# Sharing ten late rows between VectorE and GpSimd in a row-maximum kernel

## The chip, the cores and the metric

One core of a Trainium2 chip runs the kernel alone. The metric is the device time of one execution in microseconds (us). A few tenths of a microsecond lie between executions of one kernel, so a median is quoted with its range, and kernels are compared through a ratio with a 95% interval. The profile belongs to one execution and covers a slightly shorter stretch than the device time (162.6 us for 164.43 us before the change). All times inside a trace are counted from the start of that stretch.

## The reference

```
x: (32, 512, 1024) float32          # 16384 rows of 1024 numbers
out = max(x, axis=-1)               # (32, 512) float32
```

64 MiB (67.11 MB) come in, 64 KiB go out. Each of the 128 partitions owns 128 rows. In this document "a row" means one row on each partition: 128 x 1024 numbers, 512 KB.

## The kernel before

The rows come in as loads of decreasing size into a ring buffer of 46 rows. A load lands when its last byte is there. VectorE reduces each load. Near the end five full rows are spared it: TensorE turns such a row in eight 128 x 128 blocks into PSUM, ScalarE copies it back to SBUF, GpSimd takes the maximum over the partitions (an all-reduce), and TensorE turns one row of that result back into a PSUM column, from which VectorE takes a small reduction, called the merge below. The last row comes in two halves, the maximum of the first standing as one more number in front of the second.

```
BLOCKS = [[15, 15, 15, 13, 13, 11, 9, 9, 6, 6],      # rows per load
          [3, 3, 2, 1, 1, 1, 1, 1, 1, 1]]            # and one row in halves
BY_GPSIMD = {8: 1, 9: 3, 12: 1}                      # load: full rows for GpSimd
MERGE = {9: 8, 15: 9, 18: 12}                        # after load: merge of load
...
def turn(j, k):
    for c in range(C):                               # C = 8
        transpose(out=ps[:, c*P:(c+1)*P], in_=rows[:, k, c*P:(c+1)*P])   # TensorE
    nc.scalar.copy(out=sb, in_=ps)
    nc.gpsimd.partition_all_reduce(top, sb, P, max)
def back(j, k):
    for c in range(C):
        transpose(out=backs[j][:, k, c:c+1], in_=top[0:1, c*P:(c+1)*P])  # TensorE
...
for n in loads:
    nc.sync.dma_start(out=xc, in_=xb[:, b:b+n, :])
    ...
    nc.vector.reduce_max(out=cols[:, :n-m], in_=xc[:, :n-m, :])
    if j in MERGE:
        nc.vector.reduce_max(out=tiles[i][1], in_=backs[i])
...
nc.sync.dma_start(out=half, in_=xb[:, b, :H])
nc.sync.dma_start(out=tail[:, PAD:], in_=xb[:, b, H:])
nc.vector.reduce_max(out=tail[:, PAD-1:PAD], in_=half)
nc.vector.reduce_max(out=res[:, I-1:], in_=tail[:, PAD-1:])
```

## Time and profile before

| | |
|---|---|
| time, first 3 runs | 164.29 us (164.24 to 164.38) |
| loads, landings | 22; first at 21.44 us, last at 159.10 us |
| VectorE | ends at 160.36 us, 1.26 us after the last landing |
| end of the profile | 162.6 us, after the store |

### The profile page before, as it was taken

Reading aid. Unit: us, or ns where it says so; the run is one execution under the profiler, and the core shown is the slowest. Engines: PE = TensorE matmul, PEld = TensorE weight load, DVE = VectorE, ACT = ScalarE, POOL = GpSimd, SP = SyncE. Lnnn points to the kernel's source line nnn. Section 1 sums busy time; section 2 is a strip of 40 time slices with the busy share of each in tenths; the row PEclk is TensorE's granted clock in tenths of the full one; section 3 lists DMA queues with packets and bytes.
Section 4 is the critical chain, followed back from the end, with each engine's and each line's share of the span. In section 5 each row is a group of like instructions: output and inputs, shape, how many; then the busy total and the mean of one; then the engine's idle time right before and its main releaser. Section 6 shows DMA issues by size and latency. Waiting matters only on the chain.

```text
span 162.6 us, 293 instructions
## 1 busy us (share of the span) xinstructions
PE 13.0 (8%) x80; PEld 11.7 (7%) x80; DVE 135.0 (83%) x33; ACT 6.3 (4%) x6; POOL 16.3 (10%) x9
## 2 busy tenths in 40 slices
PE   0000000000000000000000000000000040943520
PEld 0000000000000000000000000000000030933420
DVE  3000079995999779999996999999999999999994
ACT  3000000000000000000000000000000011240200
POOL 0000000000000000000000000000000007099910
PEclk9999999999999999999999999999999999985555
DMA  7999699988999799999998989999999999999990
GB/s 242 484 484 438 287 484 484 484 378 348 484 484 484 333 498 432 445 419 419 419 419 387 499 388 427 417 426 408 417 435 435 471 399 426 423 418 409 406 368 16
DMA packets 3456, 67.18 MB, mean 413 GB/s; under 512 B 640, under 2 KB 640, under 8 KB 1792
## 3 DMA queue, kind: packets, MB, share of 16 engines
q1 hardware_dynamic: 3168, 67.11, 96.6%
q10 hardware_dynamic: 288, 0.07, 0.2%
HBM read 67.11 MB, written 0.07 MB: 413 GB/s over the span
## 4 chain that ended last, share of the span: by engine, by line
DVE 54%; DMA 44%; SPq 0%; issue 0%
DVE res L139 53%; DMA ring<-in_x_dram 44%; DVE res L156 0%; DVE tail L155 0%; SPq L133 0%; DVE res L143 0%
## 5 line engine op out<-in xcount | busy, mean ns | idle before, releaser
L139 DVE TENSOR_REDUCE res<-ring 128x1 f32<-128x1024 f32 (+6 forms) x20 | 132.1, 6653 | 24.3 <-DMA ring<-in_x_dram 24.3
L106 POOL PARTITION_ALL_REDUCE top<-sb x5 | 16.1, 3255 | 138.8 <-ACT sb L104 138.8
L98 PE MATMUL ps<-ident,ring 128*128 128x128 f32 x40 | 8.1, 382 | 134.2 <-DMA ring<-in_x_dram 131.8
L98 PEld LDWEIGHTS ps<-ident,ring 128*128 128x128 f32 x40 | 7.1, 204 | 134.3 <-issue 134.2
L104 ACT COPY sb<-ps 128x1024 f32<-128x1024 f32 x5 | 5.1, 1013 | 144.9 <-PE ps L98 143.0
L115 PE MATMUL fetched<-ident,top 1*128 1x1 f32 x40 | 5.0, 243 | 9.1 <-POOL top L106 9.1
L115 PEld LDWEIGHTS fetched<-ident,top 1*128 1x128 f32 x40 | 4.6, 214 | 10.3 <-POOL top L106 9.8
L104 ACT ACT_TABLE_LOAD x1 | 1.3, 1283 | 0.7 <-PEq L176 0.7
L76 DVE MEMSET ident<- 128x128 f32 x1 | 0.2, 165 | 0.8 <-PEq L176 0.8
L156 DVE TENSOR_REDUCE res<-tail 128x1 f32<-128x513 f32 x1 | 0.7, 686 | 0.0
L155 DVE TENSOR_REDUCE tail<-ring 128x1 f32<-128x512 f32 x1 | 0.7, 675 | 0.0
L83 DVE TENSOR_SCALAR rowno<-rowno 32x1 f32<-32x1 f32 x3 | 0.4, 147 | 0.1
L143 DVE TENSOR_REDUCE res<-fetched 128x1 f32<-128x8 f32 (+1 forms) x3 | 0.5, 161 | 0.0
L78 DVE TENSOR_TENSOR_SCAN colno<-ident 128x128 f32<-128x128 f32 x1 | 0.4, 425 | 0.0
L85 DVE TENSOR_SCALAR ident<-colno,rowno 128x128 f32<-128x128 f32 x1 | 0.3, 287 | 0.0
L80 DVE STREAM_TRANSPOSE rowno<-colno 128x32 f32<-128x32 f32 x1 | 0.2, 211 | 0.0
L176 POOL MEMSET const-float32-0.0<- 128x1 f32 x1 | 0.1, 99 | 0.2 <-issue 0.2
L176 POOL MEMSET const-uint8-127<- 128x1 uint8 x1 | 0.1, 103 | 0.0
L176 POOL MEMSET const-bfloat16-1.0<- 128x1 bf16 x1 | 0.1, 102 | 0.0
L176 POOL MEMSET const-float32-1.0<- 128x1 f32 x1 | 0.1, 99 | 0.0
L77 DVE MEMSET rowno<- 128x32 f32 x1 | 0.1, 85 | 0.0
## 6 DMA issues: line engine op xcount, KB each, us to landing
ring<-in_x_dram SPq DMA_DIRECT2D x3, 7680.0 KB, 38.4
ring<-in_x_dram SPq DMA_DIRECT2D x2, 6656.0 KB, 34.6
ring<-in_x_dram SPq DMA_DIRECT2D x2, 4608.0 KB, 37.8
ring<-in_x_dram SPq DMA_DIRECT2D x2, 3072.0 KB, 31.9
ring<-in_x_dram SPq DMA_DIRECT2D x1, 5632.0 KB, 28.6
ring<-in_x_dram SPq DMA_DIRECT2D x7, 512.0 KB, 22.3
ring<-in_x_dram SPq DMA_DIRECT2D x2, 1536.0 KB, 34.9
ring<-in_x_dram SPq DMA_DIRECT2D x1, 1024.0 KB, 33.4
```

The source lines that it names most:

```text
L78: in_turn("DVE", nc.vector.tensor_tensor_scan(out=colno, data0=ident, data1=ident, initial=-1.0, op0=ALU.add, op1=ALU.mult))
L83: in_turn("DVE", nc.vector.tensor_scalar(out=part, in0=part, scalar1=float(q * 32), scalar2=None, op0=ALU.add))
L85: in_turn("DVE", nc.vector.tensor_scalar(out=ident, in0=colno, scalar1=rowno[:, 0:1], scalar2=None, op0=ALU.is_equal))
L98: in_turn("PE", nc.tensor.transpose(out=ps[:, c * P:(c + 1) * P], in_=rows[:, k, c * P:(c + 1) * P], identity=ident,))
L104: nc.scalar.copy(out=sb, in_=ps)
L106: nc.gpsimd.partition_all_reduce(top, sb, P, bass_isa.ReduceOp.max)
L115: in_turn("PE", nc.tensor.transpose(out=backs[j][:, k, c:c + 1], in_=tops[j, k][0:1, c * P:(c + 1) * P], identity=ident[0:1, 0:1],))
L139: reduce = in_turn("DVE", nc.vector.reduce_max(out=cols[:, :n - m], in_=xc[:, :n - m, :], axis=X))
L143: in_turn("DVE", nc.vector.reduce_max(out=tiles[i][1], in_=backs[i], axis=X))
L155: in_turn("DVE", nc.vector.reduce_max(out=tail[:, PAD - 1:PAD], in_=half, axis=X))
L156: in_turn("DVE", nc.vector.reduce_max(out=res[:, I - 1:], in_=tail[:, PAD - 1:], axis=X))
L176: nc = _bacc.Bacc("TRN2", target_bir_lowering=False, num_devices=1)
```

## The change

The change has three parts. GpSimd takes three of eight 128-wide parts of ten late rows in place of five full rows; VectorE reduces the other five parts into one more column of the same PSUM tile, and this is written before TensorE fills the others. The load sizes change with it. The last two rows, not only the last, come in chained halves. The diff, cut to its core, with comments added (the program around it was rewritten to issue the same kind of instructions in a stated order, and its two PSUM pools have 2 and 4 buffers in place of 3 and 2):

```
 BLOCKS = [
-    [15, 15, 15, 13, 13, 11, 9, 9, 6, 6],
-    [3, 3, 2, 1, 1, 1, 1, 1, 1, 1],
+    [15, 15, 15, 13, 11, 10, 8, 6, 7, 7, 5],
+    [4, 3, 2, 2, 1, 1, 1],
 ]
-BY_GPSIMD = {8: 1, 9: 3, 12: 1}
-MERGE = {9: 8, 15: 9, 18: 12}
+SHARED = {10: (5, 3), 12: (3, 3), 14: (2, 3)}       # load: (rows, parts for GpSimd)
+MERGE = {13: (10,), 16: (12,), 20: (14,)}
...
+    # up to two rows of three parts per all-reduce, W = 768 or 384 columns
+    in_turn("POOL", nc.gpsimd.partition_all_reduce(
+        top[:, :W], sb[:, :W], P, bass_isa.ReduceOp.max))
...
+        if m and parts < C:
+            maximum(share(j)[:, parts, :], rows(j)[:, n - m:, parts * P:])
...
+    for t in range(2):
+        nc.sync.dma_start(out=half, in_=xb[:, row, :H])
+        nc.sync.dma_start(out=tails[:, t, PAD:], in_=xb[:, row, H:])
+        maximum(tails[:, t, PAD - 1:PAD], half)
+        merge(len(loads) + 2 * t)
+        last = maximum(res[:, I - 2 + t:I - 1 + t], tails[:, t, PAD - 1:])
```

More of the change, by code (lines that the diff above doesn't have):

```diff
@@ L13 @@
 BLOCKS = [
-    [15, 15, 15, 13, 13, 11, 9, 9, 6, 6],
-    [3, 3, 2, 1, 1, 1, 1, 1, 1, 1],
+    [15, 15, 15, 13, 11, 10, 8, 6, 7, 7, 5],
+    [4, 3, 2, 2, 1, 1, 1],
 ]
 RING = 46
-TENSOR = {
-    8: [("turn", 8, 0), ("back", 8, 0)],
-    9: [("turn", 9, 0), ("turn", 9, 1), ("turn", 9, 2), ("back", 9, 0)],
-    12: [("turn", 12, 0), ("back", 9, 1), ("back", 9, 2), ("back", 12, 0)],
-}
-BY_GPSIMD = {8: 1, 9: 3, 12: 1}
-MERGE = {9: 8, 15: 9, 18: 12}
+SHARED = {10: (5, 3), 12: (3, 3), 14: (2, 3)}
+TENSOR = [
+    ("turn", 10, 0), ("turn", 10, 1), ("turn", 10, 2), ("back", 10, 0),
+    ("back", 10, 1), ("turn", 12, 0), ("turn", 12, 1), ("back", 10, 2),
+    ("turn", 14, 0), ("back", 12, 0), ("back", 12, 1), ("back", 14, 0),
+]
+MERGE = {13: (10,), 16: (12,), 20: (14,)}
 NOSYNC = mybir.DependencyInfo(mybir.DependencyClass.NoSync, mybir.DependencyReason.DATA)
@@ L53 @@
     allr = ctx.enter_context(tc.tile_pool(name="allr", bufs=2))
-    psum = ctx.enter_context(tc.tile_pool(name="psum", bufs=3, space=bass.MemoryType.PSUM))
-    psmall = ctx.enter_context(tc.tile_pool(name="psmall", bufs=2, space=bass.MemoryType.PSUM))
+    psum = ctx.enter_context(tc.tile_pool(name="psum", bufs=2, space=bass.MemoryType.PSUM))
+    psmall = ctx.enter_context(tc.tile_pool(name="psmall", bufs=4, space=bass.MemoryType.PSUM))
     ring = once.tile([P, RING, D], F32)
@@ L59 @@
     PAD = 16
-    tail = once.tile([P, PAD + H], F32)
+    tails = once.tile([P, 2, PAD + H], F32)
     latest = {}
@@ L86 @@
         out=ident, in0=colno, scalar1=rowno[:, 0:1], scalar2=None, op0=ALU.is_equal))
-    tiles = {}
-    tops = {}
-    backs = {}
-    def turn(j, k):
-        rows, cols = tiles[j]
-        ps = psum.tile([P, D], F32)
-        for c in range(C):
-            in_turn("PE", nc.tensor.transpose(
-                out=ps[:, c * P:(c + 1) * P],
-                in_=rows[:, k, c * P:(c + 1) * P],
-                identity=ident,
-            ))
-        sb = turned.tile([P, D], F32)
-        nc.scalar.copy(out=sb, in_=ps)
-        top = allr.tile([P, D], F32)
-        nc.gpsimd.partition_all_reduce(top, sb, P, bass_isa.ReduceOp.max)
-        tops[j, k] = top
-    def back(j, k):
-        if j not in backs:
-            fetched = psmall.tile([P, BY_GPSIMD[j], C], F32)
-            backs[j] = fetched
-        for c in range(C):
-            in_turn("PE", nc.tensor.transpose(
-                out=backs[j][:, k, c:c + 1],
-                in_=tops[j, k][0:1, c * P:(c + 1) * P],
-                identity=ident[0:1, 0:1],
-            ))
-    at = first = j = 0
+    loads = []
+    first = at = 0
     views = []
-    for loads in BLOCKS:
-        S = sum(loads) + (loads is BLOCKS[-1])
+    for sizes in BLOCKS:
+        S = sum(sizes) + 2 * (sizes is BLOCKS[-1])
         xb = xf[first * P:(first + S) * P, :].rearrange("(p i) d -> p i d", p=P)
@@ L128 @@
         b = 0
-        for n in loads:
+        for n in sizes:
             if at + n > RING:
                 at = 0
-            xc = ring[:, at:at + n, :]
-            nc.sync.dma_start(out=xc, in_=xb[:, b:b + n, :])
-            cols = res[:, first + b:first + b + n]
-            m = BY_GPSIMD.get(j, 0)
-            tiles[j] = xc[:, n - m:, :], cols[:, n - m:]
-            for what, i, k in TENSOR.get(j, []):
-                (turn if what == "turn" else back)(i, k)
-            reduce = in_turn("DVE", nc.vector.reduce_max(
-                out=cols[:, :n - m], in_=xc[:, :n - m, :], axis=X))
-            if j in MERGE:
-                i = MERGE[j]
-                in_turn("DVE", nc.vector.reduce_max(out=tiles[i][1], in_=backs[i], axis=X))
+            loads.append((at, n, xb[:, b:b + n, :], first + b))
@@ L144, with chunks @@
             at += n
             b += n
-            j += 1
         first += S
     assert first == I
-    if at + 1 > RING:
-        at = 0
-    half = ring[:, at, :H]
-    nc.sync.dma_start(out=half, in_=xb[:, b, :H])
-    nc.sync.dma_start(out=tail[:, PAD:], in_=xb[:, b, H:])
-    in_turn("DVE", nc.vector.reduce_max(out=tail[:, PAD - 1:PAD], in_=half, axis=X))
-    in_turn("DVE", nc.vector.reduce_max(out=res[:, I - 1:], in_=tail[:, PAD - 1:], axis=X))
+    def chunks(j):
+        m, parts = SHARED[j]
+        per = max(1, C // parts)
+        return [(r, min(per, m - r)) for r in range(0, m, per)]
@@ new lines, in rows, with turn @@
+    def rows(j):
+        start, n, _, _ = loads[j]
+        return ring[:, start:start + n, :]
+    tops = {}
+    backs = {}
+    def turn(j, c):
+        m, parts = SHARED[j]
+        r, q = chunks(j)[c]
+        W = q * parts * P
+        ps = psum.tile([P, D], F32)
+        for i in range(q):
+            for c0 in range(parts):
+                k = i * parts + c0
+                in_turn("PE", nc.tensor.transpose(
+                    out=ps[:, k * P:(k + 1) * P],
+                    in_=rows(j)[:, loads[j][1] - m + r + i, c0 * P:(c0 + 1) * P],
+                    identity=ident,
+                ))
+        sb = turned.tile([P, D], F32)
+        in_turn("ACT", nc.scalar.copy(out=sb[:, :W], in_=ps[:, :W]))
+        top = allr.tile([P, D], F32)
+        in_turn("POOL", nc.gpsimd.partition_all_reduce(
+            top[:, :W], sb[:, :W], P, bass_isa.ReduceOp.max))
+        tops[j, c] = top
@@ new lines, in share, with back @@
+    def share(j):
+        m, parts = SHARED[j]
+        if j not in backs:
+            fetched = psmall.tile([P, parts + (parts < C), m], F32)
+            backs[j] = fetched
+        return backs[j]
+    def back(j, c):
+        m, parts = SHARED[j]
+        r, q = chunks(j)[c]
+        for i in range(q):
+            for c0 in range(parts):
+                k = i * parts + c0
+                in_turn("PE", nc.tensor.transpose(
+                    out=share(j)[:, c0, r + i:r + i + 1],
+                    in_=tops[j, c][0:1, k * P:(k + 1) * P],
+                    identity=ident[0:1, 0:1],
+                ))
@@ new lines, in maximum, with merge @@
+    def maximum(out, in_):
+        return in_turn("DVE", nc.vector.reduce_max(out=out, in_=in_, axis=X))
+    def merge(j):
+        for i in MERGE.get(j, ()):
+            _, k, _, c0 = loads[i]
+            q, _ = SHARED[i]
+            maximum(res[:, c0 + k - q:c0 + k], share(i).rearrange("p k m -> p m k"))
+    issued = done = 0
+    todo = list(TENSOR)
+    for j in range(len(loads)):
+        while issued < len(loads) and issued < j + 3:
+            start, n, src, _ = loads[issued]
+            held = any(s < start + n and start < s + k for s, k, _, _ in loads[j:issued])
+            if held:
+                break
+            nc.sync.dma_start(out=rows(issued), in_=src)
+            issued += 1
+        while todo and todo[0][1] < (j if todo[0][0] == "back" else issued):
+            what, i, c = todo.pop(0)
+            (turn if what == "turn" else back)(i, c)
+        _, n, _, col = loads[j]
+        m, parts = SHARED.get(j, (0, 0))
+        if n > m:
+            maximum(res[:, col:col + n - m], rows(j)[:, :n - m, :])
+        if m and parts < C:
+            maximum(share(j)[:, parts, :], rows(j)[:, n - m:, parts * P:])
+        merge(j)
@@ new lines @@
+    for what, i, c in todo:
+        assert what == "back"
+        back(i, c)
+    for t in range(2):
+        if at + 1 > RING:
+            at = 0
+        row = S - 2 + t
+        half = ring[:, at, :H]
+        at += 1
+        nc.sync.dma_start(out=half, in_=xb[:, row, :H])
[3 more added lines that the diff above has]
+        last = maximum(res[:, I - 2 + t:I - 1 + t], tails[:, t, PAD - 1:])
+        merge(len(loads) + 2 * t + 1)
+        if t == 0:
+            latest_row = last
@@ L159 @@
     store = nc.scalar.dma_start(out=views[0][0], in_=views[0][1])
-    tc.add_manual_dep(store.ins, reduce.ins.name, SYNC, reason="behind the loads")
+    tc.add_manual_dep(store.ins, latest_row.ins.name, SYNC, reason="behind the loads")
     nc.scalar.dma_start(out=views[1][0], in_=views[1][1])
```

## The prediction

> **What bounds the kernel now.** I read the slices first, then the chain of work that ended last, then the timeline of the end beside the landings. The slices:
>
> ```profile
> DVE  3000079995999779999996999999999999999994
> ...
> DMA  7999699988999799999998989999999999999990
> ```
>
> Both VectorE and the transfers are near full to the end, so the bound has to be found in single times, not in shares. The page gives 67.11 MB read at a mean of 413 GB/s over the whole span; the first three landings in the trace are at 21.44, 39.58 and 57.72 us, so 15 rows (7.86 MB) take 18.14 us, 433 GB/s. The chain:
>
> ```profile
> 21 pieces in order of time: start us, us, what
> ...
> 55.78 33.41 DMA ring<-in_x_dram
> 89.20 0.03 issue
> 89.22 53.79 DVE res L139 x6
> ...
> 157.84 1.21 DVE res L139
> 159.05 0.60 DVE tail L155
> 159.65 0.02 issue
> 159.67 0.69 DVE res L156
> ```
>
> Taken at its word this says: transfers set the time until 89.2 us, VectorE from there to the end, so that work taken off VectorE would shorten the kernel. The landings contradict it. The late one-row loads land at 155.24, 156.53 and 157.81 us, and the last one-row reductions start at 155.35, 156.55 and 157.83. The last two start 0.02 us after their data. No idle time shows, because the record of the reduction before still runs (its last 0.08 us overlap the next one). VectorE is tied to the transfers at 157.81 us and only the last row is its own:
>
> ```profile
> 157.69 0.15 DVE L143 TENSOR_REDUCE res<-fetched 128x1 f32<-128x8 f32 x1
> 157.83 1.22 DVE L139 TENSOR_REDUCE res<-ring 128x1 f32<-128x1024 f32 x1
> 158.97 0.68 DVE L155 TENSOR_REDUCE tail<-ring 128x1 f32<-128x512 f32 x1
> 159.08 0.38 ACTq L159 DMA_DIRECT2D out_dram<-res  x1
> 159.67 0.69 DVE L156 TENSOR_REDUCE res<-tail 128x1 f32<-128x513 f32 x1
> 160.39 0.34 ACTq L161 DMA_DIRECT2D out_dram<-res  x1
> ```
>
> The two halves of the last row land 9.6 us after their issue at 148.85 and 9.0 us after 150.13, in the trace at 158.48 and 159.10:
>
> ```profile
> ring<-in_x_dram SPq DMA_DIRECT2D x1, 256.0 KB, 9.6
> tail<-in_x_dram SPq DMA_DIRECT2D x1, 256.0 KB, 9.0
> ```
>
> So the last byte is there at 159.10, the last reduction could run from 159.12 to 159.81, and it ends at 160.36: **0.55 us is all that any change of VectorE's schedule can win** while the transfers stay as they are. The rest of the span (to 162.6) is the store.
>
> **What the Trainium skill says.** "DMA: Bandwidth & Descriptors", section "Where 436 GB/s comes from", puts the ceiling of the ports at 435 GB/s; the 433 GB/s above agrees, so I count on no faster transfers. "Perfetto Trace Analysis", section "Optimizing Scalar/DVE Operations", gives about 60 ns of fixed busy time for a VectorE instruction on SBUF and about 125 on PSUM, and says that the profiled latency is about twice that because the acknowledgement overlaps. The trace agrees for SBUF: a 1024-element reduction is recorded as 1.21 us but the next starts after 1.13 us, which is 1024 / 0.96 GHz = 1.07 us plus 0.06. "VectorE: DVE Perf Modes", section "The perf-mode tier table", has tensor_reduce in its slowest mode only, one element per cycle; so do these records (15360 elements, 16.15 us). "PSUM — Partial Sum Buffer", section "PSUM bank collisions raise a hardware error", asks that two engines be kept apart by bank. The new form has VectorE write one column of a PSUM tile that TensorE fills; this is presumably why its part comes first. No trace of the kernel before shows such a pair.
>
> **The change part by part.**
>
> *Transfers.* Still 22 loads and the same bytes. Landing to landing, the trace has 18.14 us for 15 rows, 15.74 for 13, 13.32 for 11, 10.92 for 9, 7.30 for 6, 3.69 for 3, 2.50 for 2, 1.28 for one and 1.30 for the two halves together: about 1.205 us per row plus 0.07 per load. The new sizes 10, 8, 7, 5, 4 then take 12.12, 9.71, 8.51, 6.10, 4.89. Summed from 21.44 the late landings are: load 9 at 132.94, load 10 at 139.04, load 11 at 143.93, load 12 at 147.62, load 13 at 150.12, load 14 at 152.62, the three single rows at 153.90, 155.18 and 156.46, the four halves at 157.11, 157.76, 158.41 and 159.06. The last byte stays where it was. I checked the ring: each new load's slot is freed long before its turn (load 14 needs load 6 reduced, at about 119 us), so nothing starves the queue.
>
> *GpSimd's share.* Before, 5 rows x 8 parts = 40 parts of 128; after, 10 rows x 3 = 30. VectorE therefore takes 10 x 5/8 - 5 = 1.25 rows **more**: 1.25 x 1.07 = 1.33 us. Its instructions stay 25 in number (20 + 3 merges + 2 before; 18 + 3 + 4 after). It can afford this because the load before 89.22 shrinks from 13 rows to 11: it lands at 86.78, before the 13-row reduction ends (87.83), so the 1.40 us of idle time there goes.
>
> *VectorE, step by step* (elements / 0.96 GHz + 0.06 us from start to start, never before landing + 0.02): load 9 waits for its landing and starts at 132.96; the 5 x 640 part of load 10 runs from 140.49 to 143.88; load 11 starts at its landing, 143.95; load 12's part at 148.28; load 13 at 150.34; merge of load 10 at 152.53 (0.09); load 14's part at 152.64; the single rows at 154.03, 155.20 and, after the merge of load 12, 156.48 (0.02 after landing). From there nothing waits: 1.13 for the row, 0.70 and 0.60 for the chained halves of the row before last, 0.59 for the next half, 0.09 for the merge of load 14, 0.69 for the last half. Sum 3.80, so VectorE ends at **160.28** instead of 160.36. The second row in halves wins nothing: two halves cost VectorE 1.30 us and the transfers 1.30 us, so the lag of about 0.5 us that it enters with stays, and one merge now stands inside that lag, where before the last merge stood inside a wait for data.
>
> *The side path must not be late.* One all-reduce of 1024 columns is:
>
> ```profile
> L106 POOL PARTITION_ALL_REDUCE top<-sb x5 | 16.1, 3255 | 138.8 <-ACT sb L104 138.8
> ```
>
> If that scales with columns, 768 take about 2.45 us and 384 about 1.25, 12.1 us in place of 16.1. Load 14 is the tight one: lands 152.62; six transposes at 0.24 us (eight took 1.94 at the reduced clock) to 154.1; the copy out of PSUM 0.8 (1.01 for 1024) to 154.9; all-reduce 155.0 to 157.5; six one-column transposes at 0.125 (eight took 1.01) to 158.4. The merge is due at 159.47: about 1.1 us to spare. Load 12's second chunk is all-reduced by about 153.7, transposed back behind load 14's turn by 155.3, and wanted at 156.33: 1.0 us to spare. Load 10 has over 2 us.
>
> *Store.* The first store's release moves from 159.05 to about 158.9, the second follows VectorE's end as before; unchanged tail.
>
> **The rivals.** (1) *A new wait on GpSimd in place of the old balance.* If an all-reduce has a large fixed cost, smaller calls save little. All five calls were the same size, so the profile cannot tell. At the extreme of 3.23 us whatever the width, load 12's second result comes at 156.4 and its merge about 0.5 us late, and load 14's last column arrives at about 160.4 for a merge due at 159.5: VectorE ends about 0.9 us later, 165.1 in all. Against it: I need only half of the cost to scale for the slack to hold. (2) *VectorE becomes the bound through small costs*: three writes into PSUM and strided input at 65 ns more each, 0.2 us, of which waits for data absorb some. End about 160.4, time 164.3 to 164.4. (3) *The whole 0.55 us is won*, if the last half is started at its landing: 163.7. Against it: the lag at 156.48 cannot be made up by halves that cost both sides 1.30. (4) *Anyone reading the chain as VectorE-bound and counting GpSimd as help* would expect VectorE relieved; it is not, it gets 1.33 us more. Nor does it get slower by 1.33, since the idle 1.40 us absorbs that.
>
> **Range and chances.** 164.29 - 0.08 = **164.2 us**. Below, the floor is 163.7, and 163.8 would need most of the lag gone; above, half of rival 1 gives 164.8. A 2% change is 3.3 us: the floor of the transfers excludes the faster side and no rival reaches the slower one. Faster 0.01, within 2% 0.98, slower 0.01.
>
> **What would show it.** In the changed trace: last landing within 0.1 us of 159.1; no idle time of VectorE at about 87 us; its late reductions starting 0.02 us after landings as late as 156.46; total VectorE busy time about 1.3 us up from 135.0; GpSimd about 12 us for six calls; the merge of load 14 following its neighbour without a gap. The prediction is wrong if a merge waits for TensorE, if the 768-column all-reduces take 3 us, if the reductions that write PSUM run slower than one element per cycle, or if the landings move, by a starved queue or by load sizes that do not follow the fit.

## More of the kernel before

VectorE's waits for loads (total us, times, longest), from the table of waits of the kernel before:

```profile
DVE res L139 <- DMA ring<-in_x_dram: 24.3, 4, 18.9
```

Its list of busy times, with the share of the span and the number of instructions:

```profile
PE 13.0 (8%) x80; PEld 11.7 (7%) x80; DVE 135.0 (83%) x33; ACT 6.3 (4%) x6; POOL 16.3 (10%) x9
```

VectorE (DVE) has 135 us of work and 24.3 us of recorded waiting for loads, most of it for the first one. How much of the work is in the way of the end cannot be read from these sums.

## The result, and the profile after

| | before | after |
|---|---|---|
| time, 6 runs each | 164.38 us (164.24 to 164.53) | 164.35 us (164.23 to 164.51) |
| first landing | 21.44 | 21.32 |
| last landing, after the first | 137.66 | 137.63 |
| VectorE's end, after the first landing | 138.92 | 138.88 |
| VectorE's end, after the last landing | 1.26 | 1.25 |

The ratio is 0.9999 (0.9986 to 1.0012): the same. The first landing differs by a tenth or more from trace to trace (21.21 to 21.46 us in eleven of the fourteen, 21.80 at most), so single traces are compared from their own first landing.

The same two lines of the changed kernel, first from its table of waits, then from its list of busy times:

```profile
DVE res L163 <- DMA ring<-in_x_dram: 22.8, 3, 18.8
```

```profile
PE 10.7 (7%) x60; PEld 9.3 (6%) x60; DVE 136.4 (84%) x33; ACT 5.3 (3%) x7; POOL 13.0 (8%) x10
```

VectorE has 1.4 us more work (136.4 against 135.0) and one wait fewer: the four waits before included the 1.40 us at 89.22 us, which is gone. The chain of waits after the change now does name the transfers in the second half (six of its 28 pieces):

```profile
57.61 41.88 DVE res L163 x3
99.50 0.02 issue
99.51 33.31 DMA ring<-in_x_dram
132.82 0.02 issue
132.84 7.62 DVE res L163
140.46 3.40 DVE fetched L163
```

Load 9 landed at 132.82 us and its reduction started 0.02 us later. The rule that a step of the chain follows what ended last has put a transfer there because VectorE happened to be free 0.05 us before. In the kernel before, the records of neighbouring reductions overlapped at such places, no wait was seen, and the chain said VectorE for the same closeness. Now the end, from the timeline (start, duration, engine and line, operation and shapes):

```profile
156.21 0.16 DVE L163 TENSOR_REDUCE res<-fetched 128x3 f32<-128x12 f32 x1
156.35 1.22 DVE L163 TENSOR_REDUCE res<-ring 128x1 f32<-128x1024 f32 x1
157.49 0.68 DVE L163 TENSOR_REDUCE tails<-ring 128x1 f32<-128x512 f32 x1
157.68 0.71 PEld L156 LDWEIGHTS fetched<-ident,top 1*128 1x128 f32 x6 [2.58 <-POOL top L138]
157.68 0.79 PE L156 MATMUL fetched<-ident,top 1*128 1x1 f32 x6 [2.49 <-POOL top L138]
158.20 0.69 DVE L163 TENSOR_REDUCE res<-tails 128x1 f32<-128x513 f32 x1
158.81 0.68 DVE L163 TENSOR_REDUCE tails<-ring 128x1 f32<-128x512 f32 x1
...
159.40 0.15 DVE L163 TENSOR_REDUCE res<-fetched 128x2 f32<-128x8 f32 x1
159.51 0.69 DVE L163 TENSOR_REDUCE res<-tails 128x1 f32<-128x513 f32 x1
```

The last one-row load landed at 156.33, its reduction started at 156.35, and from there VectorE runs to 160.20 with a single gap, of 0.03 us, before 158.20. TensorE delivers load 14's columns at 158.47 (157.68 + 0.79), 0.93 us before the merge at 159.40 asks for them.

### The profile page after: what moved, and what is told of

It reads as the page before. It is cut to its first block, busy times and chain, and to the rows that moved or that the text cites. A ratio compares the mean times of both kernels' runs of the same rounds, so it can differ in the third digit from the quotient of the medians.

```text
span 162.5 us, 266 instructions
## 1 busy us (share of the span) xinstructions
PE 10.7 (7%) x60; PEld 9.3 (6%) x60; DVE 136.4 (84%) x33; ACT 5.3 (3%) x7; POOL 13.0 (8%) x10
## 4 chain that ended last, share of the span: by engine, by line
DVE 52%; DMA 44%; another core or an unknown queue 1%; issue 1%; SPq 0%
DVE res L163 47%; DMA ring<-in_x_dram 44%; DVE fetched L163 4%; DVE tails L163 0%; SPq L180 0%
## 5 line engine op out<-in xcount | busy, mean ns | idle before, releaser
L163 DVE TENSOR_REDUCE res<-ring 128x15 f32<-128x15360 f32 (+9 forms) x15 | 125.4, 8397 | 22.9 <-DMA ring<-in_x_dram 22.8
L138 POOL PARTITION_ALL_REDUCE top<-sb x6 | 12.8, 2182 | 144.4 <-ACT sb L136 144.4
L130 PE MATMUL ps<-ident,ring 128*128 128x128 f32 x30 | 7.1, 424 | 141.8 <-DMA ring<-in_x_dram 141.8
L130 PEld LDWEIGHTS ps<-ident,ring 128*128 128x128 f32 x30 | 6.0, 224 | 141.9 <-issue 141.9
L136 ACT COPY sb<-ps 128x768 f32<-128x768 f32 (+1 forms) x6 | 4.1, 693 | 149.0 <-PE ps L130 147.6
L163 DVE TENSOR_REDUCE fetched<-ring 128x5 f32<-128x3200 f32 (+2 forms) x3 | 7.1, 2376 | 0.0
L156 PE MATMUL fetched<-ident,top 1*128 1x1 f32 x30 | 3.7, 235 | 6.0 <-POOL top L138 6.0
L156 PEld LDWEIGHTS fetched<-ident,top 1*128 1x128 f32 x30 | 3.3, 197 | 7.2 <-POOL top L138 6.9
L163 DVE TENSOR_REDUCE res<-tails 128x1 f32<-128x513 f32 x2 | 1.4, 686 | 0.0
L163 DVE TENSOR_REDUCE tails<-ring 128x1 f32<-128x512 f32 x2 | 1.4, 675 | 0.0
```

What stands on the lines that cost most here:

```text
L130: in_turn("PE", nc.tensor.transpose(out=ps[:, k * P:(k + 1) * P], in_=rows(j)[:, loads[j][1] - m + r + i, c0 * P:(c0 + 1) * P], identity=i ...
L136: in_turn("ACT", nc.scalar.copy(out=sb[:, :W], in_=ps[:, :W]))
L138: in_turn("POOL", nc.gpsimd.partition_all_reduce(top[:, :W], sb[:, :W], P, bass_isa.ReduceOp.max))
L156: in_turn("PE", nc.tensor.transpose(out=share(j)[:, c0, r + i:r + i + 1], in_=tops[j, c][0:1, k * P:(k + 1) * P], identity=ident[0:1, 0:1],))
L163: return in_turn("DVE", nc.vector.reduce_max(out=out, in_=in_, axis=X))
```

## The experiments

Two theories stood. **Theory:** the transfers set the end, with VectorE right behind them, so that work moved between VectorE and GpSimd changes nothing as long as neither is late. **Rival:** VectorE's work sets the end, as its chain of waits before reads, and the change gave back on VectorE what it won elsewhere. In the table, each time is the median of 4 to 6 runs and "before" is the kernel before in the same rounds (6 to 11 runs); the two last columns are from one trace, counted from the first landing.

| run | time | before | ratio (95%) | last landing | VectorE's end |
|---|---|---|---|---|---|
| changed kernel | 164.35 | 164.38 | 0.9999 (0.9986 to 1.0012) | 137.63 | 138.88 |
| e1 less VectorE work | 164.41 | 164.43 | 0.9996 (0.9984 to 1.0009) | 137.63 | 138.88 |
| e2 fewer bytes | 164.03 | 164.43 | 0.9974 (0.9962 to 0.9987) | 135.20 | 138.52 |
| e3 both | 161.79 | 164.43 | 0.9845 (0.9831 to 0.9860) | 135.22 | 136.47 |
| e4 two parts | 165.49 | 164.39 | 1.0070 (1.0056 to 1.0083) | 137.61 | 139.99 |
| e5 four parts | 166.93 | 164.39 | 1.0157 (1.0143 to 1.0170) | 137.64 | 141.57 |
| e6 one halved row | 164.40 | 164.43 | 1.0002 (0.9988 to 1.0015) | 137.59 | 138.84 |
| e7 no GpSimd | 167.87 | 164.39 | 1.0226 (1.0206 to 1.0247) | 137.61 | 142.50 |
| e8 before, other sizes | 164.57 | 164.39 | 1.0010 (0.9998 to 1.0023) | 137.75 | 139.00 |
| e9 18 loads | 170.04 | 164.35 | 1.0323 (1.0301 to 1.0346) | 138.42 | 143.55 |
| e10 30 transfers | 164.86 | 164.35 | 1.0032 (1.0020 to 1.0045) | 138.28 | 139.52 |
| e11 20 loads | 165.64 | 164.37 | 1.0078 (1.0065 to 1.0092) | 138.56 | 139.87 |
| e12 longer program | 164.75 | 164.38 | 1.0028 (1.0009 to 1.0047) | 137.62 | 138.88 |

### e1, e2, e3: take work from VectorE, bytes from the transfers, then both

```
 e1, e3  -            maximum(res[:, col:col + n - m], rows(j)[:, :n - m, :])
         +            k = n - m - (2 if j == 8 else 0)
         +            maximum(res[:, col:col + k], rows(j)[:, :k, :])
 e2, e3  -            nc.sync.dma_start(out=rows(issued), in_=src)
         +            k = n - (2 if issued == 8 else 0)
         +            nc.sync.dma_start(out=rows(issued)[:, :k, :], in_=src[:, :k, :])
 all     +    in_turn("DVE", nc.vector.memset(res, 0.0))      # at the start
```

> The changed kernel, but VectorE leaves out two of the seven rows of load 8 (wrong result on purpose; all bytes still come in): 2.13 us less VectorE work. Theory (the landing of the last one-row load sets the end): VectorE only waits longer at load 9 (start at 132.84 still), every later start is as before, 164.35 us within 0.15. Rival (VectorE's work sets the end, as the chain of waits reads): about 2 us less, 162.3.

> The changed kernel, but two of the seven rows of load 8 are not transferred and VectorE reduces what lay there before (wrong result on purpose): landings after load 8 about 2.4 us earlier, VectorE's work unchanged. Theory: VectorE stands right behind the transfers, so only its small waits after 57.6 us go, which add up to about 0.27 us (0.13 before load 9, 0.06 before load 11, 0.02 and 0.06 before the last single rows): 164.1. A reading in which the transfers alone set the end: 161.9.

> Both at once: the two rows of load 8 neither transferred nor reduced (wrong result on purpose). Theory: 2.4 us less from the transfers and 2.13 + 0.27 from VectorE, so 2.4 us less together, 161.95, although each alone gives next to nothing.

All three give wrong values for two of 128 rows. In e1 and e3 these are zeros (relative error 0.124). In e2 they are the maxima of two other rows, close enough for the comparison to let it pass: worked out from the input, the error is 0.019.

In e1 VectorE lost 2.13 us of work and the time did not move (164.41 against 164.43). Its timeline shows where they went, at load 9, as a wait:

```profile
110.26 20.53 DVE L164 TENSOR_REDUCE res<-ring 128x8 f32<-128x8192 f32 x3
132.98 7.62 DVE L164 TENSOR_REDUCE res<-ring 128x7 f32<-128x7168 f32 x1 [2.19 <-DMA ring<-in_x_dram]
```

In e2 the landings came 2.4 us earlier, and only 0.36 us came out at VectorE's end, a little more than the 0.27 expected from its small waits. In e3 both left and 2.41 us came out (161.79). The line of load 9 in e2, which no longer waits (it is the last of the four), and the last reductions of e2 and e3:

```profile
110.25 30.19 DVE L164 TENSOR_REDUCE res<-ring 128x8 f32<-128x8192 f32 x4
...
159.29 0.69 DVE L164 TENSOR_REDUCE res<-tails 128x1 f32<-128x513 f32 x1
...
157.04 0.69 DVE L164 TENSOR_REDUCE res<-tails 128x1 f32<-128x513 f32 x1
```

So the transfers and VectorE are at the limit together, the transfers ahead and VectorE within 0.4 us of them. Neither alone is worth much speeding up, and the rival is out: it needed 2 us from e1.

### e4, e5, e7: how the division of the rows matters

```
-SHARED = {10: (5, 3), 12: (3, 3), 14: (2, 3)}
+SHARED = {10: (5, 2), 12: (3, 2), 14: (2, 2)}   # e4, with the list of turns to match
+SHARED = {10: (5, 4), 12: (3, 4), 14: (2, 4)}   # e5
+SHARED = {}                                     # e7, no turns and no merges
```

> The changed kernel with two of eight parts of the ten rows for GpSimd in place of three: VectorE gets 10 x 128 elements more, 1.33 us. Theory: its waits absorb 0.27 us, the rest lengthens the end: 165.4. If VectorE had room to spare: 164.35.

> Four of eight parts for GpSimd: VectorE has 1.33 us less. Theory: that wins nothing, and the side path is now late: with 0.5 us + 2.61 ns per column (from the 768 and 384 column calls, 2.50 and 1.50 us) the six all-reduces take 3.2 us for 1024 and 1.84 for 512 columns, load 12's merge waits about 1.9 us and load 14's last, end about 2.2 us later: 166.5. Rival (VectorE's work sets the end): 163.0.

> The changed kernel with nothing for GpSimd; VectorE reduces all 128 rows. Theory: 3.75 rows more are 4.0 us, less 0.27 us for three merges and 0.27 us of waits absorbed: about 3.5 us more, 167.8. If the transfers alone set the end: 164.4.

Two parts cost 1.11 us at VectorE's end (139.99 - 138.88; 1.06 expected), none at all 3.62 us (3.5 expected): VectorE has no room for more. With four parts it has 1.33 us less to do and its end comes 2.69 us later (141.57 - 138.88; 2.2 expected). Its timeline names the cause:

```profile
152.84 0.18 DVE L163 TENSOR_REDUCE res<-fetched 128x5 f32<-128x25 f32 x1 [0.57 <-PE fetched L156]
...
158.45 0.17 DVE L163 TENSOR_REDUCE res<-fetched 128x3 f32<-128x15 f32 x1 [2.05 <-PE fetched L156]
...
162.09 0.17 DVE L163 TENSOR_REDUCE res<-fetched 128x2 f32<-128x10 f32 x1 [0.42 <-PE fetched L156]
```

All three merges wait for TensorE, which waits for GpSimd. The first wait, of 0.57 us, was not expected. The six all-reduces take 16.4 us in total; the first starts at 142.20 and the last ends at 160.99, where the changed kernel wanted load 14's result at 159.40. This was the prediction's first rival, and four parts is where it comes true. Three parts lie between a VectorE that is too full and a GpSimd that is too late, which makes this division a good one without making it faster than the old one.

### e6: only the last row in halves

```
-    [4, 3, 2, 2, 1, 1, 1],
+    [4, 3, 2, 2, 1, 1, 1, 1],
-MERGE = {13: (10,), 16: (12,), 20: (14,)}
+MERGE = {13: (10,), 16: (12,), 19: (14,)}
-    for t in range(2):
+    for t in range(1):                           # row = S - 1
```

> The changed kernel with only its last row in halves, as the kernel before has it; the row before comes as one load. Theory: halves of a row cost VectorE and the transfers 1.30 us each, so halving a second row wins nothing: end 0.0 to 0.1 us earlier than the changed kernel, one load fewer, 164.3. Rival (the second pair of halves shortens the lag at the end): about 0.5 us slower, 164.8.

The time is 164.40 us, against 164.43 for the kernel before, and VectorE ends 138.84 us after the first landing, against 138.88 in the changed kernel: the second pair of halves is worth nothing.

### e8: the kernel before with its 1.40 us of idle time taken away

```
-    [15, 15, 15, 13, 13, 11, 9, 9, 6, 6],
+    [15, 15, 15, 13, 11, 10, 8, 7, 6, 6, 6],
-BY_GPSIMD = {8: 1, 9: 3, 12: 1}
+BY_GPSIMD = {9: 1, 10: 3, 13: 1}                # the same rows' share, one load later
```

> The kernel before (five full rows for GpSimd) with first-block loads of 15, 15, 15, 13, 11, 10, 8, 7, 6, 6, 6 rows, which takes away its 1.40 us of VectorE idle at 89.2 us and adds one load. Theory: the freed VectorE time is lost again in waits for later landings, the added load costs 0.07 us: 164.4 to 164.5. Rival (VectorE-bound from 89.2 us on, as its chain reads): about 1.3 us less, 163.1.

The wait at 89.2 us was gone and three others stood in its place:

```profile
138.93 3.35 DVE L140 TENSOR_REDUCE res<-ring 128x3 f32<-128x3072 f32 x1 [0.77 <-DMA ring<-in_x_dram]
142.19 0.16 DVE L144 TENSOR_REDUCE res<-fetched 128x1 f32<-128x8 f32 x1
142.62 3.35 DVE L140 TENSOR_REDUCE res<-ring 128x3 f32<-128x3072 f32 x1 [0.27 <-DMA ring<-in_x_dram]
146.31 7.86 DVE L140 TENSOR_REDUCE res<-ring 128x3 f32<-128x3072 f32 x5 [0.33 <-DMA ring<-in_x_dram]
```

0.77 + 0.27 + 0.33 = 1.37 us. The time was 164.57 against 164.39, a little above the 164.4 to 164.5 expected, and the interval includes no difference. The 1.40 us that the change used for GpSimd's smaller share was free time, worth nothing by itself.

### e10: the cost of a load

```
-            nc.sync.dma_start(out=rows(issued), in_=src)
+            cuts = [0, n // 2, n] if 1 <= issued <= 8 else [0, n]
+            for a, b in zip(cuts, cuts[1:]):
+                nc.sync.dma_start(out=rows(issued)[:, a:b, :], in_=src[:, a:b, :])
```

> The changed kernel with each of loads 1 to 8 sent as two transfers into the same place; VectorE still waits for both and does the same work. Theory: eight transfers more at 0.07 us each push the last landing and the end back by about 0.55 us: 164.9. If the number of transfers does not matter and only bytes do: 164.35.

Eight more transfers of the same bytes moved the last landing from 137.63 to 138.28 us after the first, 0.08 us each, and VectorE's end by 0.64 us with it (139.52 - 138.88). The time rose to 164.86. VectorE's work was the same; it waited longer at load 9:

```profile
133.35 7.62 DVE L163 TENSOR_REDUCE res<-ring 128x7 f32<-128x7168 f32 x1 [0.42 <-DMA ring<-in_x_dram]
```

The transfers do set the end.

### e9 and e11: two tries to beat both kernels with fewer loads

```
 e9   [15, 15, 15, 15, 15, 15, 12, 8], [5, 3, 3, 2, 1, 1, 1]; the last two rows as one
      load of both first halves, then two halves
      SHARED = {4: (6, 8), 5: (5, 3), 6: (3, 8), 7: (2, 8), 8: (2, 8), 10: (2, 3), 11: (2, 3)}
 e11  [15, 15, 15, 15, 14, 12, 10, 10, 6], [4, 3, 2, 2, 1, 1, 1]
      SHARED = {7: (3, 8), 8: (5, 3), 10: (3, 3), 12: (2, 3)}
```

> A try to beat both: GpSimd also takes full rows of earlier loads (18.5 rows less VectorE work than none, against 3.75), which lets the loads be coarser (18 instead of 22: six of 15 rows, then 12, 8, 5, 3, 3, 2, 1, 1, 1, a pair of half rows, two halves). Theory: each load costs the transfers about 0.07 us, so the last landing comes about 0.3 us earlier, and the end with it: 164.1. If the number of loads does not matter: 164.35.

> A smaller try than the one with 18 loads, with the side path put right: three full rows of load 7 go to GpSimd besides the ten shared rows (230 instead of 134 TensorE instructions, turns ordered ahead of the fetches), and the freed 3.2 us of VectorE pay for coarser loads: 20 in place of 22 (15, 15, 15, 15, 14, 12, 10, 10, 6, then 4, 3, 2, 2, 1, 1, 1 and the halves). Theory: two loads fewer at 0.08 us each, end about 0.17 us earlier than the changed kernel: 164.2, ratio to the kernel before about 0.9985. If the side path is late again or an instruction fetch falls among the loads: 165 or more.

The figure of 18.5 rows in the expectation of e9 was a slip: by the table of shares 13 full rows and 9 x 3/8 go to GpSimd, 16.4 in all.

Both failed. First, the side path (TensorE, ScalarE, GpSimd and TensorE again) was late: in e9 one merge waits 2.21 us and another 1.46 us for TensorE, to which the program gives its instructions in a fixed order and which once stood 5.6 us, before turning a result back into a PSUM tile, until VectorE had written its own part there. In e11 two merges wait:

```profile
153.28 0.18 DVE L165 TENSOR_REDUCE res<-fetched 128x5 f32<-128x20 f32 x1 [0.58 <-PE fetched L158]
...
157.52 0.17 DVE L165 TENSOR_REDUCE res<-fetched 128x3 f32<-128x12 f32 x1 [0.42 <-PE fetched L158]
...
160.04 0.68 DVE L165 TENSOR_REDUCE tails<-ring 128x1 f32<-128x512 f32 x1
```

These two waits, 1.00 us together, account for e11's end, 0.99 us after that of the changed kernel (139.87 - 138.88). In e9 the two waits are 3.67 us of 4.67. Second, the landings came late, which nothing in the plan explains. Both traces have a queue that no trace before them has; the page of e9, with the queue's name, packets and megabytes:

```profile
q1 hardware_dynamic: 2720, 67.11, 93.1%
q10 hardware_dynamic: 288, 0.07, 0.2%
q8 instruction: 2, 0.03, 0.1%
```

In e9 one such packet of 16 KB started at 120.75 us and took 0.99 us, and the 12-row load then in flight landed 15.64 us after its predecessor. The same size of load took 14.54 us in e11: 1.10 us late. In e11 such a packet started at 156.94 us and took 1.09 us, and a half row landed 1.71 us after its predecessor in place of the usual 0.67. Twice, then, a load that was in flight during such a packet, which this document takes for a fetch of instructions by the kind of its queue, landed about 1.1 us late, and all later ones with it. That this made the kernels slower is not shown. In e11 it did not move VectorE's end: the late half landed at 159.52 us, and VectorE, held up by the merges, came to it only at 160.04 (the last line above). The second packet of e9, at 159.24 us, delayed nothing that shows: the last two halves landed 0.65 and 0.62 us after their predecessors. No version that is faster than the two kernels and gives all the maxima was found.

### e12: a longer program and nothing else

```
+    ps = psum.tile([P, D], F32)
+    for q in range(48):
+        in_turn("PE", nc.tensor.transpose(out=ps[:, :P], in_=ident, identity=ident))
```

> The changed kernel with 48 needless transposes of the identity on TensorE at the start, long before any data is there, so that TensorE's program is as long as in the try with 20 loads (230 recorded matmuls and weight loads instead of 134). Nothing else changes. Theory from that try: the trace shows a 16 KB packet on an instruction queue after some 207 to 219 of TensorE's instructions, here at about 154 to 157 us, and the load in flight then lands about 1.05 us late: about 165.4. If the longer program costs nothing: 164.35.

A packet of 16 KB did appear, but in the profiled execution at 163.5 us, after the last load and after the last profiled instruction (the span is 162.7 us), and this execution took 164.46 us, like the kernel before. The six runs split into 164.17, 164.46, 164.52 and 164.99, 165.18, 165.24 us, where the kernel before stayed between 164.23 and 164.51. That would fit a fetch that falls among the loads in some executions and behind them in others, but only one trace was taken, and it is of the faster kind. The record speaks against it for one of the three slower runs: their spans are 163.2, 162.7 and 163.5 us, and the one of 165.18 us has the span of the faster runs, so its extra time lies outside the profiled instructions. Nor is the length of the program all that changed: the mean granted TensorE clock is 0.55 in all six runs, against 0.95 to 0.96 for the kernel before. It is the same in the faster and the slower runs, so it does not tell them apart. The expected time of the fetch was wrong. That this longer program is slower on average than the kernel before is shown (1.0028, 1.0009 to 1.0047); it was not run beside the changed kernel, and what slows the three runs stays open.

## Why the prediction was right

- **What bounds the kernel.** Right, and shown by e1, e2, e3 and e10. The reading that mattered was the 0.02 us between landing and start at 156.53 and 157.81 us, against a chain of waits that said VectorE. The prediction says that the record before overlaps by 0.08 us there; at these two starts it overlaps by 0.01 us only, so VectorE was held back by 0.07 us each time. The section that it cites for 435 GB/s ("DMA: Bandwidth & Descriptors", "Where 436 GB/s comes from", of the Trainium skill) also says that for loads from HBM a lower limit binds, about 358 GB/s; the 433 GB/s measured here lies above that, and the prediction leaves this out.
- **Transfers unchanged.** Right: 137.63 us from first to last landing, 137.66 before; 137.62 had been worked out (159.06 - 21.44). The sign named for it, a last landing within 0.1 us of 159.1 in the trace, failed as worded: it came at 158.95, because the first landing came 0.12 us earlier.
- **VectorE: 1.33 us more work, 1.40 us less waiting.** Right: busy time rose by 1.4 us and the wait at 89 us went. e8 shows that this time was free.
- **VectorE's end.** 160.28 was predicted from a first landing at 21.44, that is 138.84 after it; it came 138.88 after it. The gain of 0.08 us was 0.03 us in the medians and is not distinguishable from none. (Its own sums put load 14's merge at 159.50, not 159.47.)
- **The second row in halves wins nothing.** Right (e6).
- **GpSimd's time.** This term was mis-sized: "If that scales with columns, 768 take about 2.45 us and 384 about 1.25, 12.1 us in place of 16.1". Four and two calls of these times would make 12.3, not 12.1. The calls took 2.50 and 1.50 us, 12.8 us in all. A call has a fixed part. Both calls of 384 columns here follow another call directly, and the record of such a call is 0.08 us longer (768 columns: 2.58 in place of 2.50). Calls that start alone took 1.43 us for 384 columns (e9), 1.79 for 512 (e4), 2.50 for 768 and 3.22 for 1024 (the kernel before): 2.81 ns per column and about 0.35 us besides (2.50 - 768 x 2.81 ns). The 0.5 us in the expectation of e5 came from mixing the two kinds. Load 14's merge had 0.93 us to spare instead of 1.1 (the longer call is 0.05 us of the difference), so nothing came of it. The lines of the two groups, from the changed kernel's list of groups (count, busy us, mean ns, idle before):

```profile
L138 POOL PARTITION_ALL_REDUCE top<-sb x6 | 12.8, 2182 | 144.4 <-ACT sb L136 144.4
...
L163 DVE TENSOR_REDUCE fetched<-ring 128x5 f32<-128x3200 f32 x1 | 3.5, 3484 | 0.0
```

- **VectorE as the bound through small costs** (second rival). It did not come. The second line above is VectorE's strided part of load 10 with its output in PSUM: 3484 ns, which is 3200 / 0.96 GHz = 3333 ns and 151 ns more (14336 elements more take 16153 - 1210 ns more in the reductions into SBUF, which is 0.96 elements per ns), the same excess as the 1024-element reductions into SBUF have (1210 - 1067 = 143 ns).
- **The whole 0.55 us is won** (third rival). It did not come: VectorE ends 1.25 us after the last landing, as before 1.26. The lag is made when a full row is reduced in 1.13 us while the next half lands after 0.67 us.

The absolute time, 164.2 us, was taken from three runs with a median of 164.29; with six the kernel before stands at 164.38, which accounts for most of the distance to 164.35.

## What to carry to other kernels

Where an engine starts each piece of work a few hundredths of a microsecond after its data lands, it is tied to the transfers even if no idle time is recorded and the chain of waits names the engine; look at landings beside starts before moving work. When two resources run level, taking from either alone gives little (0.02 and 0.40 us against the kernel before, where both together gave 2.64), and an experiment that takes from both, beside one for each, shows it in three runs. Free time in the middle of a kernel can pay for work that is moved, but it is no gain by itself.

## What the Trainium skill lacked or had wrong

- "Runtime: NRT & Kernel Launch", section "Instruction fetch mechanics", calls the cost of crossing a 16 KiB boundary of the program "mostly hidden". It does not say what such a fetch does to loads in flight. Four packets of 16 KB on an instruction queue are in the traces of e9, e11 and e12. Three of them started before the last load had landed, and during two of these, of 0.99 and 1.09 us, the load in flight landed 1.10 and 1.04 us late (15.64 for 14.54, 1.71 for 0.67). That the packet was the cause was not tested, and in e11 the late landing did not move VectorE's end.
- "DMA: Bandwidth & Descriptors", section "Anatomy of one DMA — SWDGE (gpsimd) path", gives about 2 us of fixed cost for a DMA. It has no figure for loads that are queued one behind another from SyncE: there each costs 0.08 us (eight more moved the last landing by 0.65 us).
- "GPSIMD Engine Reference", section "3.2 Cross-partition — where GPSIMD wins", gives 247.7 us for a reduction over partitions at [128, 2048]. It does not have the partition all-reduce, which took 1.43, 2.50 and 3.22 us for 384, 768 and 1024 columns where the call started alone.
- "Perfetto Trace Analysis", section "Optimizing Scalar/DVE Operations", gives about 125 ns of fixed time where VectorE uses PSUM. With the output alone in PSUM no extra was seen (151 ns of recorded excess against 143), and merges that read 8 and 20 numbers from PSUM let the next instruction start after 0.07 us (8 numbers, at 142.93 us in the kernel before) and 0.08 us (20 numbers, at 152.43 us in the changed kernel).
